# Head-output sums and values' low parts on GpSimd, and reordered steps beside the retention matmuls

## The chip, the cores and the metric

The kernel runs on one core of one Trainium2 chip. The time is the device time of one execution in microseconds (us); the kernel before takes 1518.18 us, the median of 3 runs (1517.76 to 1519.46). Engine names are those of the profile: PE (TensorE matmul, with PEld for its weight loads), DVE (VectorE), ACT (ScalarE), POOL (GpSimd) and SP (SyncE, which here only issues transfers).

## The reference

One layer of a hybrid model on a batch of 1: a feed-forward block, a mixer and a second feed-forward block, each behind an RMS norm and with a residual. The sequence has 512 tokens behind 16 meta tokens, the model width is 1024, everything is float32. The mixer adds two branches, each weighted with a sigmoid gate:

```
proj = u @ w_in          # split into rq, rk, rv, rg, aq, ak, av, iq, ik, iw, g_ret, g_att
rq = rope(rq); rk = rope(rk) * 256 ** -0.5            # 4 heads of 256, values of 512
yr = retention(rq, rk, rv)                            # decayed q k^T times v, RMS-normed per head
yr = (silu(rg) * yr) @ w_ret_out
qi, ki = rope(iq), rope(ik)                           # 8 index heads of 64, one key
score = sum_h wi[h] * relu(qi[h] @ ki)                # causal; the best 128 keys of each query
ya = dsa_attention(aq, ak, av, selected keys) @ w_att_out     # 8 heads of 128
merged = sigmoid(g_ret) * yr + sigmoid(g_att) * ya
return merged @ w_mix_out
```

The retention's recurrence over chunks equals one causal product with a matrix of decays, and the kernel computes it in that form.

## The kernel before

**Split matmuls.** Each float32 operand is split into a high part, rounded to the format that PE reads (`fp32r`), and a low part, the operand minus the high part. ACT writes the high part (`whi`, `vh`, `o`, `ikh`) and DVE the low one (`wlo`, `vl`, `ikl`). A product is three matmuls: high by high, high by low, low by high (`mm3`, L155).

**The order.** In the part that the change touches, the order on PE, DVE and ACT is the order in which the code is written. A list of steps (`more`) goes through a pipeline: each step is a weight tile, whose high part is made ahead of time and whose low part is made by `lower()`, and a function that emits the matmuls and then the work "beside" them. `between=((k, op), ...)` emits `op` before the k-th of the eight contraction steps of a projection; `behind` runs after it. An engine works through its own instructions in this order and stops at the first whose input is missing, so a late transfer or a long operation holds everything that is written behind it on that engine. SP and POOL issue transfers in their own written order. PSUM has two double banks and four single banks (`sm_tile`); a product waits when the banks have not been emptied.

**The retention stage** lies between 624 and 945 us of the span. Its steps are:

1. Gates 0 and 1 of the retention branch (`psgate`), with the loads of head 0 and of the index tables.
2. `decayed(0)`: query-key products of head 0 (`psst`), times the decay table (DVE, L1542), split into `ph` and `pl`. Its values are split by `values_in` (L1487 to L1493).
3. Projections of head 1's queries and keys (`psrq`, `psrk`). Beside the first lies `weigh_all(0)`: the products with the values (`pspv`, L1563, four blocks b of b + 1 key blocks), a sum of squares on ACT, and a product with the gate on DVE (`g<-pspv,g`, L1569). Each half of the result is normed and transposed in 32 x 32 blocks (`turn`), and goes through DRAM (`ots`) back into `land`.
4. Gates 2 and 3, with the index scores between them: one `pair` fills two banks with score products (`pssc`, L1315), followed by a relu on ACT into one of four `tmp` buffers (L1319) and a weighted sum on DVE (L1322). Their operands `iq`, `ikh` and `ikl` come from `index_queries` (four steps) and `index_keys` (three).
5. `arrived(0)` splits what landed into `o` (L322 and L323, one operation on each engine for each half).
6. Per head: `outputs(h)`, four steps of two products `psro` (one row block of `w_ret_out` each), added into eight accumulators `accr` in SBUF (L1694 to L1722; ACT copies for h = 0 at L1710, DVE adds otherwise at L1712). Inside the same steps lie `values_in(h+1)`, `decayed(h+1)` and `weigh_all(h+1)`. Then `queries_keys(h+2)` (L1663 to L1690) with the turned halves of head h+1, and so on. The last head has the projections of the attention's first key and query (`psak`, `psaq`) and gates 4 and 5 instead.
7. Between these, `pick(n)` emits n steps of the selection of the best keys, each a MAX (L1334) and a MATCH_REPLACE (L1335) on DVE over one score tile. There are 48 such steps in all.

The attention's heads come after it. For the last head the probabilities are transposed on PE (`psPT`, L1989 to L2002), split, and multiplied with the values (`weigh_v`, `psao`) inside the first column of the output projection (`psat`).

The lines that set the order of the retention stage:

```
more += queries_keys(1, (beside_q0, beside_q1, beside_k0, nothing), ((), (), (), ((7, pair),)))
five = tuple((i, pair) for i in (1, 2, 4, 5, 7))
more += steps_of(gr[2:4], [proj("psgate", REAL, five, after_2), proj("psgate", REAL, five, after_3)])
for h in range(1, RH - 1):
    more += outputs(h - 1, beside_outputs(h - 1))
    more += queries_keys(h + 1, (lambda h=h: (trip(h), pick(2)), lambda: pick(1), ...))
```

## Time and profile before

| | |
|---|---|
| median of 3 runs | 1518.18 us |
| the profiled execution's own time | 1518.44 us |
| its span | 1516.5 us |
| PE busy | 1483.9 us, 98% |
| DVE busy | 1143.6 us, 75% |
| ACT busy | 750.5 us, 49% |
| POOL busy | 192.7 us, 13% |
| mean granted clock of PE | 0.992 |
| retention, 600 to 950 us: PE, DVE, ACT, POOL busy | 330.4, 274.7, 169.9, 34.7 of 350 us |

A row of a timeline gives the start, the duration, the engine, the line and operation, what it writes and reads, its shape, a count where neighbours of one kind were joined, and in brackets the idle time before it with what ended it. A group row gives the same for all instructions of one kind: their number, then busy time and the mean of one in ns. Matmuls are pipelined: a duration of 0.39 us in a row stands beside starts that lie 0.23 us apart. A window row gives the busy times of the five engines, the mean granted clock of PE (1.00 is full), the busy share of the DMA engines and GB/s.

### The profile page before, as it was taken

The numbers are of one execution on the slowest core, as the hardware profiler recorded it, in microseconds if no ns is written. First come the engines' busy times: TensorE is split into PE (matmuls) and PEld (weight loads), VectorE is DVE, ScalarE is ACT, GpSimd is POOL, SyncE is SP. The second block draws the span as 40 slices with busy tenths as digits, with TensorE's granted clock in tenths as the row PEclk, the third lists the DMA queues.
The fourth block names the chain that finished last, engine by engine and source line by source line (L and its number), as shares of the span: only waits on it lengthen the run. The fifth ranks groups of instructions, "written<-read, shape, count | busy, mean of one in ns | idle before, by whom it ended". The sixth has DMA issues, their size and how long they took to land.

```text
span 1516.5 us, 22282 instructions
## 1 busy us (share of the span) xinstructions
PE 1483.9 (98%) x8704; PEld 1300.1 (86%) x8704; DVE 1143.6 (75%) x1715; ACT 750.5 (49%) x1054; POOL 192.7 (13%) x288
## 2 busy tenths in 40 slices
PE   9999999999999999989999999999999999999997
PEld 8999999999988778877878878989788888888886
DVE  5988586786887887477888878888557787777776
ACT  5555263455354444455543427677534644434343
POOL 1000000002100000210000002444202321111110
PEclk9999999999999999999999999999999999999999
DMA  5232323226654443544335344666657476466322
GB/s 169 69 123 85 116 90 106 97 89 214 220 169 142 157 166 120 197 149 150 114 136 171 114 149 121 172 178 178 208 164 261 150 228 205 127 206 198 123 84 110
DMA packets 185272, 228.41 MB, mean 151 GB/s; under 512 B 34768, under 2 KB 131560, under 8 KB 184912
## 3 DMA queue, kind: packets, MB, share of 16 engines
q1 hardware_dynamic: 164768, 173.97, 35.8%
q0 software_dynamic: 16288, 45.67, 10.3%
q10 hardware_dynamic: 4112, 7.36, 1.4%
q8 instruction: 68, 1.11, 0.3%
q14 instruction: 36, 0.29, 0.1%
HBM read 187.17 MB, written 39.60 MB: 150 GB/s over the span
## 4 chain that ended last, share of the span: by engine, by line
PE 86%; DVE 9%; ACT 3%; issue 2%; DMA 0%; POOL 0%; POOLq 0%; DVEq 0%; ACTq 0%
PE psd L155 8%; PE psd L2447 8%; PE psqX L2282 7%; PE psqX L155 7%; PE psvX L1196 7%; PE psvY L1196 4%; PE psqY L2282 4%; PE psqY L155 3%; PE psga L155 3%; PE psat L155 3%; PE psmo L155 3%; PE psak L155 3%; PE psaq L155 3%; PE psgate L155 2%; PE psrq L155 2%; PE psro L155 2%
## 5 line engine op out<-in xcount | busy, mean ns | idle before, releaser
L322 ACT ACTIVATE whi<-raw 128x1024 fp32r<-128x1024 f32 (+2 forms) x142 | 133.5, 941 | 125.0 <-PE psd L155 41.2
L323 DVE TENSOR_TENSOR wlo<-raw,whi 128x1024 fp32r<-128x1024 f32 (+2 forms) x142 | 155.8, 1100 | 34.0 <-ACT whi L322 34.0
L323 DVE TENSOR_TENSOR wlo<-w,whi 128x1024 fp32r<-128x1024 f32 x96 | 116.9, 1219 | 64.4 <-ACT whi L322 64.3
L322 ACT ACTIVATE whi<-w 128x1024 fp32r<-128x1024 f32 x96 | 101.5, 1058 | 110.1 <-PE psd L2447 39.3
L155 PE MATMUL psro<-o,whi 128*128 128x512 f32 x256 | 81.9, 400 | 6.5 <-DVE o L323 4.8
L155 PE MATMUL psd<-hl,whi 128*128 128x264 f32 x352 | 71.3, 284 | 0.0
L155 PE MATMUL psd<-hh,wlo 128*128 128x264 f32 x352 | 70.8, 283 | 0.0
L155 PE MATMUL psd<-hh,whi 128*128 128x264 f32 x352 | 70.7, 282 | 0.0
L155 PEld LDWEIGHTS psro<-o,whi 128*128 128x128 f32 x256 | 49.4, 193 | 18.6 <-DVE o L323 5.8
L115 ACT ACTIVATE whi<-raw 128x1024 fp32r<-128x1024 f32 (+1 forms) x42 | 43.5, 1036 | 42.4 <-PE psat L155 9.9
L155 PE MATMUL psqX<-tl,whi 128*128 128x264 f32 x216 | 61.1, 283 | 0.0
L155 PE MATMUL psqX<-th,whi 128*128 128x264 f32 x216 | 61.1, 283 | 0.0
L155 PE MATMUL psqX<-th,wlo 128*128 128x264 f32 x216 | 61.1, 283 | 0.0
L116 DVE TENSOR_TENSOR wlo<-raw,whi 128x1024 fp32r<-128x1024 f32 (+1 forms) x42 | 50.9, 1215 | 9.7 <-ACT whi L115 9.7
L2447 PE MATMUL psd<-whi,hl 128*128 128x512 f32 (+1 forms) x148 | 56.9, 384 | 0.0
L2447 PE MATMUL psd<-whi,hh 128*128 128x512 f32 (+1 forms) x148 | 56.8, 383 | 0.0
L2447 PE MATMUL psd<-wlo,hh 128*128 128x512 f32 (+1 forms) x148 | 56.7, 383 | 0.0
L155 PEld LDWEIGHTS psd<-hh,wlo 128*128 128x128 f32 x352 | 54.4, 188 | 0.0
L155 PEld LDWEIGHTS psd<-hh,whi 128*128 128x128 f32 x352 | 54.1, 188 | 0.0
L155 PEld LDWEIGHTS psd<-hl,whi 128*128 128x128 f32 x352 | 54.0, 188 | 0.0
L322 ACT ACTIVATE whi<-wsum 128x1024 fp32r<-128x1024 f32 x36 | 38.1, 1059 | 30.5 <-PE psd L155 15.0
L155 PE MATMUL psro<-o,wlo 128*128 128x512 f32 x128 | 50.9, 398 | 0.0
(566 smaller groups left out, 4701.5 us busy)
## 6 DMA issues: line engine op xcount, KB each, us to landing
w<-in_w_in_dram SPq DMA_DIRECT2D x40, 512.0 KB, 5.1
raw<-in_w_in_dram SPq DMA_DIRECT2D x27, 512.0 KB, 3.9
raw<-in_w_in_dram SPq DMA_DIRECT2D x13, 1024.0 KB, 6.0
raw<-in_ffn_w_down_dram SPq DMA_DIRECT2D x24, 512.0 KB, 4.0
raw<-in_ffn_w_up_dram SPq DMA_DIRECT2D x11, 1024.0 KB, 5.1
raw<-in_ffn_w_gate_dram SPq DMA_DIRECT2D x10, 1024.0 KB, 5.0
ws<-in_ffn_w_up_dram POOLq DMA_DIRECT2D x20, 512.0 KB, 6.4
w<-in_ffn_w_up_dram SPq DMA_DIRECT2D x20, 512.0 KB, 5.5
```

The costliest lines, as they stand in the source:

```text
L115: nc.scalar.activation(hi, src, AF.Copy)
L116: eng.tensor_tensor(lo, src, hi.bitcast(F32), ALU.subtract)
L155: nc.tensor.matmul(o, a[:, k, :], b[:, sl], start=first and k == 0 and i == 0, stop=last and k == nk - 1 and i == 2, skip_group_check=onto)
L322: nc.scalar.activation(hi, src, AF.Copy)
L323: return lambda: nc.vector.tensor_tensor(lo, src, hi.bitcast(F32), ALU.subtract)
L1196: nc.tensor.matmul(d[bank_][t], a, b[:, k, :], start=not onto and j + k + m == 0, stop=j + k == 3 and m == 2, skip_group_check=onto)
L2282: nc.tensor.matmul(ps[:, t], a, b[:, k, :], start=not onto and j + k + m == 0, stop=j + k == 3 and m == 2, skip_group_check=onto)
L2447: nc.tensor.matmul(ps, a, m[:, j, cs], start=first and i == 0, stop=last and i == 2)
```

## The change

1. **Index operands.** SP loads the index tables before the index queries' tile; the other four pieces of that tile are issued from POOL earlier. The multiplies and the addition of the index key, and its low part, go from DVE to POOL. The first two steps of `index_queries` are written right behind `decayed(0)`, the third beside head 1's second query projection, and the fourth ahead of the two rope steps beside the key projection.
2. **Values.** Head 0's values are split inside gate 1, before contraction step 4. For the other heads the low part is subtracted on POOL instead of DVE.
3. **Turns.** Two of the four transfers of each second half are issued from POOL.
4. **Accumulation.** Each `psro` bank is emptied by a copy on ACT, directly behind its matmuls and ahead of `lower()` and the steps beside. For h = 0 the copy goes into the accumulator; otherwise into one of two halves of `RR`, and POOL adds it to the accumulator.
5. **Scores and halves.** Score pairs begin inside the last key projection and lie at other contraction steps of gates 2 and 3. Both halves of head 0's `o` are split inside gate 2; both halves of heads 1 and 2 come beside the first key projection, with no selection step between; those of head 3 come inside gates 4 and 5.
6. **Selection.** The selection steps are distributed anew: before there were places for 54, so that the last places had none left; now there are places for 45, and the last three steps come at the end of the stage.
7. **Attention's end.** Three of the last head's four transposed blocks lie inside the projection before them, in free tiles, and the last weighing comes two contraction steps earlier in the first output column.

DVE around the weighing of head 0: before, from the last piece of the decays (`ptail`) on.

```order
L1379 TENSOR_TENSOR ptail<-tmp,ptail 16x512 [waits Activation_49]
L1493 TENSOR_TENSOR vl<-vl,vh 128x1024 [waits DMAHW1_49,Activation_49]
L1493 TENSOR_TENSOR vl<-vl,vh 128x1024 [waits DMAHW2_49,Activation_49]
L323 TENSOR_TENSOR wlo<-raw,whi 128x1024 [waits DMAHW7_49,Activation_49]
L1454 TENSOR_TENSOR tmp<-tmp,cos 64x512 [waits DMAHW6_49,DMASW5_49]
L1455 TENSOR_TENSOR tmp<-tmp,sin 64x512 [waits DMAHW7_49,DMASW7_49,DMASW6_49]
L1457 TENSOR_TENSOR tmp<-tmp 64x512 [waits DVE_49]
L1462 TENSOR_TENSOR ikl<-tmp,ikh 64x512 [waits Activation_49] x2
L1569 TENSOR_TENSOR g<-pspv,g 128x512 [waits Activation_49] x2
```

And in the changed kernel, from the same row:

```order
L1379 TENSOR_TENSOR ptail<-tmp,ptail 16x512 [waits Activation_49]
L1442 TENSOR_TENSOR ixs<-ixs,cos 128x4x384 [waits DMAHW7_49,DMAHW5_49]
L1442 TENSOR_TENSOR ixs<-ixs,sin 128x4x384 [waits DMASW4_49,DMASW3_49,DMAHW6_49,DMASW2_49,DMASW1_49]
L323 TENSOR_TENSOR wlo<-raw,whi 128x1024 [waits Activation_49]
L1570 TENSOR_TENSOR g<-pspv,g 128x512 [waits Activation_49] x2
L1574 TENSOR_SCALAR osum<-osum 128x2
```

`vl` now stands ahead of the decays, the index key is gone from DVE, and the two multiplies of the index queries (`ixs`), which wait for transfers, stand ahead of the weights' low part and of the gate products that empty the `pspv` banks.

ACT in the outputs of head 1, with the last rope pieces of head 2's keys and head 2's values and decays: before, no copy of a `psro` bank is on ACT here.

```order
L322 ACTIVATE rqk<-tmp 128x528
L322 ACTIVATE whi<-raw 128x1024
L322 ACTIVATE rqk<-tmp 128x528
L1491 ACTIVATE vh<-vraw 128x1024 x2
L322 ACTIVATE whi<-raw 128x1024
L1498 ACTIVATE g<-g 128x1024 x2
L322 ACTIVATE ph<-tmp 128x512
```

In the changed kernel:

```order
L1712 ACTIVATE RR<-psro 128x512
L322 ACTIVATE rqk<-tmp 128x528
L1712 ACTIVATE RR<-psro 128x512
L322 ACTIVATE whi<-raw 128x1024
L1712 ACTIVATE RR<-psro 128x512
L322 ACTIVATE rqk<-tmp 128x528
L1712 ACTIVATE RR<-psro 128x512
L1491 ACTIVATE vh<-vraw 128x1024 x2
L322 ACTIVATE whi<-raw 128x1024
L1712 ACTIVATE RR<-psro 128x512
L1499 ACTIVATE g<-g 128x1024 x2
L1712 ACTIVATE RR<-psro 128x512
```

A copy now stands ahead of a high part of the weights each time, and one copy stands behind the two Silu passes (`g<-g`). POOL's additions follow these copies one for one, with the two low parts of the values after the fourth.

DVE beside the first key projection of head 2, with head 1's landed halves: before, from the second rope piece on.

```order
L323 TENSOR_TENSOR rqk<-tmp,rqk 128x512 [waits Activation_49]
L323 TENSOR_TENSOR o<-land,o 128x4x256 [waits DMAHW0_49,Activation_49]
L1334 MAX top<-score_6588 128x8
L1335 MATCH_REPLACE score_6588<-top,score_6588 128x512 [waits DVE_49]
L1334 MAX top<-score_6588 128x8 [waits DVE_49]
L1335 MATCH_REPLACE score_6588<-top,score_6588 128x512 [waits DVE_49]
L323 TENSOR_TENSOR wlo<-raw,whi 128x1024 [waits PE_49,Activation_49]
L323 TENSOR_TENSOR o<-land,o 128x4x256 [waits DMAHW1_49,Activation_49]
```

In the changed kernel:

```order
L323 TENSOR_TENSOR wlo<-raw,whi 128x1024 [waits DMAHW1_49,Activation_49]
L323 TENSOR_TENSOR o<-land,o 128x4x256 [waits DMAHW4_49,Activation_49]
L323 TENSOR_TENSOR o<-land,o 128x4x256 [waits DMAHW5_49,Activation_49]
L323 TENSOR_TENSOR rqk<-tmp,rqk 128x512 [waits DVE_49]
L1519 TENSOR_TENSOR tmp<-tmp 128x512 [waits DVE_49]
L323 TENSOR_TENSOR rqk<-tmp,rqk 128x512 [waits Activation_49]
L323 TENSOR_TENSOR wlo<-raw,whi 128x1024 [waits PE_49,Activation_49]
```

Both halves now stand next to each other, ahead of the last rope pieces and of the selection steps.

The diff, cut to its core:

```diff
         def bring_index():
-            nc.sync.dma_start(ia[:, :, :NL], fq[:, :, :NL])
-            for r in range(4):
-                o = r ^ 1
-                nc.gpsimd.dma_start(ib[32 * r : 32 * r + 32, :, :NL], fq[32 * o : 32 * o + 32, :, :NL])
             for i, t in enumerate((cosi, sini)):
                 nc.sync.dma_start(t, rope[0, i, :, REAL])
+            nc.sync.dma_start(ia[:, :, :NL], fq[:, :, :NL])
...
+            PT = nc.gpsimd.tensor_tensor
             if i == 0:
-                TT(a, a, cosi[:64], ALU.mult)
-                TT(b, b, sini[:64], ALU.mult)
-            elif i == 1:
-                TT(a, a, b, ALU.add)
+                PT(a, a, cosi[:64], ALU.mult)
+                PT(b, b, sini[:64], ALU.mult)
+                PT(a, a, b, ALU.add)
...
+            low = nc.gpsimd.tensor_tensor if h else TT
             for i in range(2):
-                TT(lo[i].bitcast(F32R), lo[i], hi[:, 2 * i : 2 * i + 2].bitcast(F32), ALU.subtract)
+                low(lo[i].bitcast(F32R), lo[i], hi[:, 2 * i : 2 * i + 2].bitcast(F32), ALU.subtract)
...
-                nc.sync.dma_start(d.rearrange("(b i) a e -> a i b e", i=32)[a],
+                eng = nc.gpsimd if half and a > 1 else nc.sync
+                eng.dma_start(d.rearrange("(b i) a e -> a i b e", i=32)[a],
...
             def k0(ps):
                 pss["ka"] = ps
+                asides[2]()
                 some(ropes["q"], 2)
-                asides[2]()
...
-                        if j == 0:
-                            lower()
-                            beside(i)
                         a = acc_r[2 * i + j]
                         if h == 0:
                             nc.scalar.activation(a, ps, AF.Copy)
                         else:
-                            TT(a, ps, a, ALU.add)
+                            t = RR[:, j * S : (j + 1) * S]
+                            nc.scalar.activation(t, ps, AF.Copy)
+                            nc.gpsimd.tensor_tensor(a, a, t, ALU.add)
+                        if j == 0:
+                            lower()
+                            beside(i)
...
-                pick((1, h == 0, 1 + (h == 0), 2 + (h == 0))[i])
+                pick((1, 1, 0, 1)[i])
...
-            values_in(0)
+            index_queries(0)
+            index_queries(1)
+            index_keys(0)
...
-            proj("psgate", REAL, (), after_1)(w, lower)
+            proj("psgate", REAL, ((4, lambda: values_in(0)),), after_1)(w, lower)
...
-        more += queries_keys(1, (beside_q0, beside_q1, beside_k0, nothing), ((), (), (), ((7, pair),)))
-        five = tuple((i, pair) for i in (1, 2, 4, 5, 7))
-        more += steps_of(gr[2:4], [proj("psgate", REAL, five, after_2), proj("psgate", REAL, five, after_3)])
+        more += queries_keys(1, (beside_q0, beside_q1, beside_k0, nothing), ((), (), (), ((3, pair), (7, pair))))
+        come = [(i, lambda half=half: arrived(0, (half,))) for half, i in enumerate((2, 6))]
+        more += steps_of(gr[2:4], [proj("psgate", REAL, (*come, *((i, pair) for i in (1, 3, 5, 7))), later_gate(2)),
+                                   proj("psgate", REAL, tuple((i, pair) for i in (0, 2, 4, 6, 7)), after_3)])
...
-            more += queries_keys(h + 1, (lambda h=h: (trip(h), pick(2)), lambda: pick(1), lambda h=h: (arrived(h, (0,)), pick(2)),
-                                           lambda h=h: (arrived(h, (1,)), pick(2))))
+            more += queries_keys(h + 1, (lambda h=h: (trip(h), pick(3)), lambda: pick(1), lambda h=h: arrived(h), lambda: pick(2)))
...
-        more += steps_of(gr[4:6], [proj("psgate", REAL, (), lambda ps: (later_gate(4)(ps), arrived(p, (0,)), pick(4))),
-                                   proj("psgate", REAL, (), lambda ps: (later_gate(5)(ps), arrived(p, (1,)), pick(4)))])
+        more += steps_of(gr[4:6], [proj("psgate", REAL, ((6, lambda: arrived(p, (0,))),), lambda ps: (later_gate(4)(ps), pick(2))),
+                                   proj("psgate", REAL, ((2, lambda: arrived(p, (1,))),), lambda ps: (later_gate(5)(ps), pick(3)))])
...
-                    wide_gate()
+                    ends = last_tiles()
+                    wide_gate(between=[(3 + i, lambda kb=kb: transpose_block(kb, ends[kb])) for i, kb in enumerate((0, 1, 3))])
...
-                between=((KD - 1, lambda: weigh_v(AH - 1, pend, vs[AH - 1])),))
+                between=((KD - 3, lambda: weigh_v(AH - 1, pend, vs[AH - 1])),))
```

More of the change, by code (lines that the diff above doesn't have):

```diff
@@ L1862, with gate_a @@
     ga = Cols(w_in, OFF_GA, KD, step=1)
-    def gate_a(ps):
-        mm3([(ps, REAL)], ga.next(), xs, KD)
+    def gate_a(ps, between=()):
+        mm3([(ps, REAL)], ga.next(), xs, KD, between=between)
         t = tp["pool"].tile([P, S], F32, tag="gate", name="gate", bufs=2)
@@ L1987, in weigh_turned, with transpose_block, transpose_tail @@
                 split(*(t.rearrange(f"p ({o}) -> p a j c", a=4, j=4) for o, t in zip(("a j c", "j a c", "j a c"), (ps, *ao_parts[h]))))
[L1989 to L1997 removed]
+            def transpose_block(kb, parts):
+                ps = sm_tile("psPT")
+                for j in range(kb, 4):
+                    nc.tensor.transpose(ps[:, j * P : (j + 1) * P], prob[j][:, NM + kb * P : NM + (kb + 1) * P], ident)
+                split(ps[:, kb * P :], *parts)
+            def transpose_tail():
                 ps = sm_tile("psPT")
@@ L2001, in transpose_p, with last_tiles @@
                 split_rows(ps[:NM], tp["p"], "hlh")
-                return parts
+            def transpose_p():
+                parts = [part_tiles(kb, S - kb * P) for kb in range(4)]
+                for kb in range(4):
+                    transpose_block(kb, parts[kb])
+                transpose_tail()
+                return parts
+            def last_tiles():
+                a, b = ([at.tile([P, n], F32R, tag=f"a{t}{i}", name="ptx") for i in range(2)] for t, n in (("q", S), ("k", TX)))
+                return [a, [t[:, : S - P] for t in b], part_tiles(2, 2 * P), [t[:, S - P : S] for t in b]]
             def weigh_v(h, parts, v):
@@ L2012, in weigh_v, with wide_gate @@
                 split(ps, *ao_parts[h])
-            def wide_gate(tile=None):
+            def wide_gate(tile=None, between=()):
                 if gr.at < gr.n:
@@ L2017, in wide_gate @@
                 else:
-                    t = gate_a(tile or mm_tile("psga")[:, :S])
+                    t = gate_a(tile or mm_tile("psga")[:, :S], between)
                     nc.sync.dma_start(gd[KD + ga.at - 1], t)
```

39 lines of the change are left out of this document (15 added, 24 removed).

## The prediction

> **What bounds the kernel now.** I read four views in this order: the totals and the chain of waits, to see which engine sets the end; what TensorE (PE) waited for in the stage that the change rewrites; the granted clock there; and single rows on DVE, ACT and POOL for prices. First the totals and the chain:
>
> ```profile
> PE 1483.9 (98%) x8704; PEld 1300.1 (86%) x8704; DVE 1143.6 (75%) x1715; ACT 750.5 (49%) x1054; POOL 192.7 (13%) x288
> ...
> PE 86%; DVE 9%; ACT 3%; issue 2%; DMA 0%; POOL 0%; POOLq 0%; DVEq 0%; ACTq 0%
> ```
>
> PE is the bound, and no matmul is added or dropped. So the change can gain only PE's idle time and matmuls that ran at a reduced clock. The whole span has 1516.5 - 1483.9 = 32.6 us idle. The next view lists the waits of PE from 600 to 950 us, where the retention stage lies (columns: engine, tile and line of the waiting matmul, what released it, sum of us, count, longest):
>
> ```profile
> PE psro L155 <- DVE o L323: 4.8, 3, 2.0
> PE pssc L1315 <- DVE iq L1449: 3.2, 2, 2.1
> PE pssc L1315 <- ACT tmp L1319: 2.8, 1, 2.8
> PE psst L1538 <- DVE accr L1712: 1.7, 2, 1.4
> PE psro L155 <- ACT o L322: 1.7, 1, 1.7
> PE psst L1538 <- ACT accr L1710: 1.4, 1, 1.4
> PE pspv L1563 <- ACT vh L1491: 1.2, 1, 1.2
> PE pspv L1563 <- DVE vl L1493: 0.8, 1, 0.8
> PE pspv L1563 <- DVE accr L1712: 0.7, 2, 0.5
> PE pspv L1563 <- DVE g L1569: 0.6, 1, 0.6
> ```
>
> These sum to 18.9 us, and every one has an edit aimed at it. Now the stretches around the long waits (columns: busy of PE, weight load, DVE, ACT, POOL, then PE's granted clock, DMA share, GB/s):
>
> ```profile
> 644.00:656.00 12.00, 9.39 (x33) 6.68 (x31) 7.93 (x10) 8.20 (x13) 0.83 (x1) 0.86 0.65 210
> ...
> 676.00:684.00 8.00, 4.82 (x16) 3.33 (x15) 6.15 (x5) 6.01 (x7) 0.00 (x0) 0.79 0.06 9
> ...
> 884.00:896.00 12.00, 8.90 (x27) 6.55 (x26) 11.45 (x32) 2.56 (x3) 0.55 (x1) 0.72 0.42 153
> ...
> 692.00:704.00 12.00, 9.18 (x41) 7.73 (x40) 8.34 (x12) 7.83 (x13) 0.58 (x1) 0.86 0.06 22
> ...
> 700.00:950.00 250.00, 238.98 (x1211) 200.77 (x1211) 208.47 (x387) 117.94 (x178) 19.83 (x32) 0.98 0.45 141
> ```
>
> The clock is below full in the first four. Length times (1 - clock) is what was lost: 12 x 0.14 = 1.7, 8 x 0.21 = 1.7, 12 x 0.28 = 3.4 and 12 x 0.14 = 1.7, together 8.5 us. Single rows show what such a loss looks like, and where it doesn't come:
>
> ```profile
> 679.20 0.50 PE L1315 MATMUL pssc<-ikh,iq 128*128 128x512 f32 x1 [2.12 <-DVE iq L1449]
> ...
> 680.99 0.80 PE L1315 MATMUL pssc<-ikh,iq 128*128 128x512 f32 x1 [1.06 <-DVE iq L1449]
> ...
> 682.01 0.63 PE L155 MATMUL psgate<-xh,whi 128*128 128x512 f32 x1
> ...
> 766.71 0.50 PE L155 MATMUL psro<-o,whi 128*128 128x512 f32 x1 [1.96 <-DVE o L323]
> 767.05 0.40 PE L155 MATMUL psro<-o,wlo 128*128 128x512 f32 x1
> ```
>
> After 3.2 us of idle close together a matmul of 512 columns took 0.63 us; after one idle of 1.96 us it still took 0.40. The four stretches hold 2.0 to 3.2 us of idle close together (the waits of the list, added by place). So a removed wait is worth more than its length where idle time is dense. The Trainium skill (TensorE: Matmul & The Clock Gate, the part on the clock gate) says that an idle window of about 3.4 us, free-running, halves the clock; by it alone a stage with idle below that keeps its clock, and the clock losses here could also fall elsewhere in a run. The rows agree in that one idle of 1.96 us cost nothing; they differ in that losses came below 3.4 us of idle. I count the clock as recoverable, and keep the other case as a rival.
>
> **The change, place by place.** DVE, ACT and POOL prices first, from groups and single rows (start, duration, engine, line, operation):
>
> ```profile
> L1712 DVE TENSOR_TENSOR accr<-psro,accr 128x512 f32<-128x512 f32 x16 | 10.2, 681 | 0.0
> L1493 DVE TENSOR_TENSOR vraw<-vraw,vh 128x1024 fp32r<-128x1024 f32 x6 | 7.1, 1217 | 0.0
> L1710 ACT ACTIVATE accr<-psro 128x512 f32<-128x512 f32 x8 | 4.4, 586 | 0.9 <-PE psro L155 0.9
> L1396 POOL TENSOR_TENSOR accr<-accr,gate 128x512 f32<-128x512 f32 x8 | 11.2, 1394 | 37.3 <-DMA gate<-gd 20.8 <-ACT gate L2026 9.0 <-ACT gate L1392 7.5
> ...
> 648.96 0.83 POOL L1330 COPY bias<-caus 128x128 f32<-128x128 f32 x1 [7.95 <-DMA caus<-in_causal_dram]
> ...
> 647.28 2.36 DVE L1493 TENSOR_TENSOR vl<-vl,vh 128x1024 fp32r<-128x1024 f32 x2 [4.24 <-ACT vh L1491]
> ...
> 663.39 1.72 DVE L1442 TENSOR_TENSOR ixs<-ixs,cos 128x1536 f32<-128x1536 f32 x1
> 665.03 1.75 DVE L1442 TENSOR_TENSOR ixs<-ixs,sin 128x1536 f32<-128x1536 f32 x1
> ...
> 645.47 0.39 PE L155 MATMUL psrq<-xl,whi 128*128 128x512 f32 x1
> 645.70 0.39 PE L155 MATMUL psrq<-xh,wlo 128*128 128x512 f32 x1
> ...
> 658.75 0.40 PE L155 MATMUL psrq<-xh,whi 128*128 128x512 f32 x1
> ```
>
> Work moved: DVE loses 24 accumulations (24 x 0.68 = 16.3 us) and six low parts (6 x 1.22 = 7.3). ACT gains 24 copies (24 x 0.59 = 14.2), hidden while ACT is busy 117.9 of 250 us. POOL gains 24 x 1.39 = 33.4 and six low parts; the trace has no 128x1024 on POOL, so I take twice 1.39, 2.8 each, 16.7 together (bounds 1.39, and 3.0 by the slowest 128x512 shown below). That is 50 us on an engine busy 19.8 of those 250. It is hidden unless a copy has to wait for its half of RR. Five index-key operations of 64x512 go to POOL too; I cost them at nothing, since POOL is busy 0.83 of 12 us in the first stretch and the first score comes 20 us later; without that cover the scores would wait for them.
>
> A, head 0's weighing (644 to 660). Splitting the values inside gate 1 removes the waits on vh and vl (1.2 + 0.8) and, with them, the 1.7 of clock. But DVE's queue now holds the two index multiplies (1.72 + 1.75) and the weights' low part (1.22, row in D) ahead of the first g, and they wait for index loads. The table issued just behind those loads landed at 648.96, the latest row for them; the queries' own tile now comes third, and I take 647 for it (an estimate, two us ahead of that row since its bytes stand ahead of the table's). Then the first g is done at 647 + 3.5 + 1.2 + 0.7 = 652.4. PE would reach block 3 of the weighing at 650.8: the waits end, four matmuls of block 0, seven and ten more, at the 0.23 us by which the two psrq rows follow each other, from 645.9. It waits 1.6, finishes block 3 (13 x 0.23 = 3.0) at 655.4 and starts the next projection 3.3 us sooner than at 658.75. Bounds: 4.9 with no wait; 1.3 if the load comes at 648.96. I take 3.3.
>
> B, first index scores (676 to 684). The queries' multiplies are done about 12 us sooner, and their low parts stand ahead of the rope steps. Both waits (3.2) and the 1.7 of clock go; the moved steps may hold the rope pieces by up to 1.7 on DVE, in front of matmuls of a later head: I take 4.7, bounds 1.5 (the clock stays) and 4.9.
>
> C, gates 2 and 3 (692 to 704). The 2.8-us wait sat behind DVE's two halves of `o`, 2.36 us in one piece, so ACT could not refill its four temporaries. Now the halves go in one at a time between score pairs. DVE still has 4 x 1.22 of weights, 2.4 of halves and 24 weighted sums in about 19 us of PE work, so I expect 1.0 left: 2.8 + 1.7 - 1.0 = 3.5, bounds 1.0 and 4.5.
>
> D, the gaps of 0.3 to 2.0 us between outputs and heads. What is left of the list of waits is psro <- DVE o without its last (4.8 - 1.4 = 3.4), psst and pspv <- accr (1.7 + 1.4 + 0.7 = 3.8): 7.2 us. The rows behind the largest of them:
>
> ```profile
> 764.30 1.22 DVE L323 TENSOR_TENSOR wlo<-raw,whi 128x1024 fp32r<-128x1024 f32 x1
> 765.43 1.22 DVE L323 TENSOR_TENSOR o<-land,o 128x1024 fp32r<-128x1024 f32 x1
> ```
>
> The second half was queued behind three selection steps; both halves now stand ahead of them. ACT's copies free a bank without DVE's selection in front of it, but one bank still waits behind two Silu passes. I take 6.0 of 7.2, bounds 3 and 7.2.
>
> E, the last head (884 to 896): two waits of 1.7 and 1.4 and 3.4 of clock, 6.5. The halves move into gates 4 and 5, several us ahead of their use, and two of the second turn's four transfers leave SP's queue for POOL's, where at most one addition of 1.39 stands ahead of them. I take 6.0, bounds 3.1 and 6.5.
>
> F, the attention tail, from these PE rows:
>
> ```profile
> 1084.17 0.60 PE L2000 MATMUL psPT<-ident,pj 128*16 128x128 f32 x4 [0.92 <-DVE ptl L116]
> ...
> 1092.53 0.50 PE L155 MATMUL psat<-vo,whi 128*128 128x512 f32 x1 [0.69 <-ACT vo L115]
> 1093.26 0.50 PE L155 MATMUL psat<-vo,whi 128*128 128x512 f32 x1 [0.22 <-DVE vo L116]
> ```
>
> Three of the transposes now lie inside a projection, and the last weighing is two steps earlier: 1.4 of 1.8, bounds 0 and 1.8.
>
> The sum is 3.3 + 4.7 + 3.5 + 6.0 + 6.0 + 1.4 = 24.9. Against it stands what POOL does to DVE, from rows of DVE and then POOL:
>
> ```profile
> 951.74 2.19 DVE L116 TENSOR_TENSOR wlo<-raw,whi 128x1024 fp32r<-128x1024 f32 x1
> ...
> 951.35 1.50 POOL L1294 TENSOR_TENSOR tmp<-tmp,sin 128x512 f32<-128x512 f32 x1 [1.80 <-DVE cross L1953]
> ```
>
> The split that elsewhere takes 1.22 took 2.19 beside 1.1 us of POOL's multiply: almost the whole overlap is lost. POOL's new 50 us over PE's 250 would meet DVE operations that read two SBUF tiles for about 40% of the time (weights, halves, rqk and low parts), and cost 50 x 0.4 x 0.9 = 18 us of DVE. DVE is relieved of 23.6, so it stays below its 208 of 250; but single late splits will come. I charge one new idle of the present mean, 18.9 / 15 counted waits = 1.3, and one clock loss of 1.7, together 3. The Trainium skill (GPSIMD Engine Reference, specifications and key points) speaks against this change: the two engines share their SBUF interfaces when DVE has two SBUF inputs, and it puts elementwise work on POOL at about half DVE's rate. The trace agrees on both (2.19 for 1.22, 1.39 against 0.68), and by that page alone the move would gain nothing on DVE; the gains above come mostly from order, not from DVE's total.
>
> So 24.9 - 3 = 22 us. Against the profiled execution's own 1518.44 (span 1516.5 and 1.9 around it), within 0.3 of the median shown, that gives 1496.5; I round to **1497**.
>
> **Rivals.** First, the idle moves instead of going: A's load comes at 648.96 or later and the wait before g keeps its clock loss, C stays bound by DVE, D gives half. With the lower bounds of A to F, 1.3 + 1.5 + 1.0 + 3.0 + 3.1 + 0 = 9.9, the time is about 1508. DVE's 83% of 700 to 950 us speaks for it; against it, the waits sit behind named operations that leave.
>
> Second, the clock windows stay though the waits are shorter: 24.9 - 8.5 - 3 = 13.4, about 1505. A new idle of 1.6 us in A after the present dense stretch would be where it starts; the 1.96 us without loss speaks against it.
>
> Third, no net change. POOL's 18 us of stretch all land before PE (bank-emptying copies, RR halves and splits), and eat the 22: 1514 to 1520. That needs DVE to be the bound nearly throughout; it has more than 20 us of reserve per 250.
>
> Fourth, **slower**: the copy of output pair i waits on ACT until POOL's addition has read RR's half. Each copy now stands ahead of the weight splits in ACT's queue, so a POOL queue that is late by x makes ACT, the weights and PE late by x. It decides once POOL needs more than PE's time for an output: 12 matmuls of 0.23 = 2.7 us against 1.39, or 2.8 after a low part. Two low parts (5.6) sit in POOL's queue between the fourth and fifth addition of each of two heads, and the copy after next would wait 5.6 + 1.39 - 2 x 2.7 = 1.6 there. If each of the 24 copies waited that much, 24 x 1.6 = 38 against 24.9 of gain: 1518.4 + 13 = 1531. Only three such places have low parts, so it needs POOL twice as slow as in its rows.
>
> **How the numbers follow.** Forecast 0.58; idle moved 0.18; clock stays 0.10; no net change 0.07; slower 0.07. The first three are faster by over 0.2% (3 us, about what a measurement of this kernel can tell from no change), and so lies their sum, 0.86; the rest is shared as 0.07 and 0.07. The forecast's upper gain is the sum of the upper bounds, 4.9 + 4.9 + 4.5 + 7.2 + 6.5 + 1.8 = 29.8, which gives 1488.6. For the low end I take 1489, for the high end 1509, which takes in the first two rivals.
>
> **What would show it.** Right: PE's idle between 600 and 950 below 4 us, the clock 1.00 in 676 to 704 and 884 to 896, no psro wait on `o`, no psst wait on an accumulation. For A: a wait of pspv on g of 1 to 2 us before block 3. Wrong: a clock below 0.9 in any of the four stretches, ACT waiting on POOL's accr rows, DVE's splits above 1.6 us in the outputs, or pspv waiting on the index multiplies for over 2.5 us. A PE busy sum above 1484 would mean slower matmuls, which nothing here counts on.

## The result and the profile after

The changed kernel takes 1495.57 us (median of 4 runs, 1494.3 to 1496.16) against 1518.82 us before (4 runs, 1517.76 to 1519.65): a ratio of 0.9846, 95% interval 0.9829 to 0.9863. The forecast was 1497 in a range of 1489 to 1509. The profiled execution took 1496.16 us, its span is 1494.4.

First its totals and its chain of waits (shares of the span by engine):

```profile
PE 1476.2 (99%) x8704; PEld 1296.7 (87%) x8704; DVE 1130.1 (76%) x1680; ACT 761.6 (51%) x1078; POOL 261.9 (18%) x331
...
PE 92%; DVE 3%; DMA 2%; ACT 2%; issue 1%; POOL 0%; POOLq 0%; ACTq 0%; SPq 0%; DVEq 0%
```

PE's idle time fell from 32.6 to 18.2 us, and its busy time by 7.7 us with the same 8704 matmuls. Most of the latter is clock: 8.5 us were lost in the retention stage before, 1.8 now. DVE's busy time fell by only 13.5 us, though work of 27 us left it (16.3 of accumulations, 7.3 of low parts, 3.4 of the index key). The waits of PE between 600 and 950 us:

```profile
PE pspv L1564 <- DVE g L1570: 2.9, 1, 2.9
PE psst L1539 <- DVE tmp L1543: 1.0, 1, 1.0
PE pssc L1315 <- ACT wt L1302: 0.9, 1, 0.9
PE pssc L1315 <- ACT tmp L1319: 0.7, 1, 0.7
```

Every wait on `o`, on an accumulation, and on `vh` and `vl` is gone, and those on `iq` are down from 3.2 to 0.2 us. One new wait stands out: 2.9 us on `g`. The window view shows where the time went (PE, weight load, DVE, ACT, POOL, granted clock, DMA share, GB/s):

```profile
644.00:656.00 12.00, 9.22 (x41) 7.29 (x39) 9.40 (x9) 7.76 (x13) 6.99 (x8) 1.00 0.77 258
656.00:676.00 20.00, 19.84 (x118) 17.80 (x119) 13.63 (x19) 10.14 (x13) 6.91 (x9) 0.91 0.57 153
...
700.00:950.00 250.00, 249.27 (x1305) 212.96 (x1304) 211.04 (x398) 141.07 (x221) 86.97 (x78) 1.00 0.50 156
```

From 700 to 950 us PE stops for 0.7 us in all; before it stopped for 11. The weighing of head 0 still has its stop, and the 656 to 676 window lost 20 x 0.09 = 1.8 us of clock behind it. Its rows on PE and DVE (start, duration, and in brackets the idle time before with its releaser):

```profile
656.16 0.80 PE L1564 MATMUL pspv<-vh,ph 128*128 128x512 f32 x1 [2.94 <-DVE g L1570]
656.75 0.63 PE L1564 MATMUL pspv<-vl,ph 128*128 128x512 f32 x1
...
649.78 1.76 DVE L1442 TENSOR_TENSOR ixs<-ixs,cos 128x1536 f32<-128x1536 f32 x1 [1.93 <-DMA ixs<-fq]
651.46 1.85 DVE L1442 TENSOR_TENSOR ixs<-ixs,sin 128x1536 f32<-128x1536 f32 x1
653.23 2.28 DVE L323 TENSOR_TENSOR wlo<-raw,whi 128x1024 fp32r<-128x1024 f32 x1
655.43 1.27 DVE L1570 TENSOR_TENSOR g<-pspv,g 128x512 f32<-128x512 f32 x2
...
651.66 2.76 POOL L1457 TENSOR_TENSOR tmp<-tmp 64x512 f32<-64x512 f32 x1
```

DVE stood 1.93 us for the index load, and the weights' split then took 2.28 us beside POOL's 2.76-us addition of the index key, where it takes 1.22 alone.

The table gives the time by place: how much later (+) or sooner (-) a kernel passes each stretch than the kernel before, from the start times of the same matmuls in both traces. A runs from the first gate to head 1's second query projection, B and C from there to the first output, D to gate 4, E to gate 6, F to the end of the span. The runs below are in it.

| kernel | A | B, C | D | E | F |
|---|---|---|---|---|---|
| predicted | -3.3 | -8.2 | -6.0 | -6.0 | -1.4 |
| changed | +0.9 | -7.2 | -8.9 | -6.5 | -1.4 |
| changed, again | -0.9 | -7.2 | -8.9 | -6.5 | -0.9 |
| index_behind | -3.2 | -3.0 | -8.9 | -6.5 | -2.2 |
| index_between | -2.8 | -3.0 | -8.9 | -6.5 | -2.4 |
| between_psw | -3.8 | -2.0 | -8.9 | -6.5 | -2.0 |
| iq_early | -3.8 | -5.0 | -8.9 | -6.5 | -1.8 |
| accr_dve | -0.6 | -7.2 | -8.9 | -6.5 | +3.9 |
| accr_late | -0.8 | -7.2 | -0.4 | -6.5 | -1.4 |
| halves_old | -0.7 | -4.2 | -3.7 | -0.2 | -2.4 |
| vl_dve | -0.9 | -7.3 | -7.5 | -6.5 | -2.3 |
| attn_old | +0.8 | -7.2 | -8.9 | -6.5 | +0.5 |
| relief_alone | +1.6 | -0.6 | 0.0 | -2.7 | +0.2 |
| halves_alone | 0.0 | +1.3 | -5.5 | -6.5 | +7.3 |

B to E repeat within 0.1 us wherever their code is the same. A and F do not. Seven of the traces have the changed kernel's code in A (both of the changed kernel, `accr_dve`, `accr_late`, `halves_old`, `vl_dve`, `attn_old`), and in all seven the load of the index queries lets DVE start 23.9 to 24.3 us behind the first gate. Five of them have an A of -0.6 to -0.9. The other two, at +0.8 and +0.9, lost clock behind the wait on `g`. F varies from -0.9 to -2.4 us with the same code, and why is open. The spans start up to 1.5 us apart ahead of A, in code that no run touches.

### The profile page after: what moved, and what is told of

Read it like the earlier page. It is cut to its first block, busy times and chain, and to the rows that moved or that the text cites. A ratio compares the mean times of both kernels' runs of the same rounds, so it can differ in the third digit from the quotient of the medians.

```text
span 1494.4 us, 22333 instructions
## 1 busy us (share of the span) xinstructions
PE 1476.2 (99%) x8704; PEld 1296.7 (87%) x8704; DVE 1130.1 (76%) x1680; ACT 761.6 (51%) x1078; POOL 261.9 (18%) x331
## 4 chain that ended last, share of the span: by engine, by line
PE 92%; DVE 3%; DMA 2%; ACT 2%; issue 1%; POOL 0%; POOLq 0%; ACTq 0%; SPq 0%; DVEq 0%
PE psd L155 8%; PE psqX L2293 7%; PE psd L2458 7%; PE psqX L155 7%; PE psvX L1196 7%; PE psro L155 6%; PE psvY L1196 4%; PE psqY L2293 4%; PE psqY L155 3%; PE psat L155 3%; PE psmo L155 3%; PE psak L155 3%; PE psaq L155 3%; PE psrk L155 2%; PE psgate L155 2%; PE psrq L155 2%
## 5 line engine op out<-in xcount | busy, mean ns | idle before, releaser
L323 DVE TENSOR_TENSOR wlo<-raw,whi 128x1024 fp32r<-128x1024 f32 (+2 forms) x142 | 160.2, 1131 | 36.3 <-ACT whi L322 36.0
L155 PE MATMUL psro<-o,whi 128*128 128x512 f32 x256 | 78.9, 389 | 0.0
L287 POOL TENSOR_TENSOR RR<-RR,sq 128x528 f32<-128x528 f32 x7 | 9.4, 1336 | 324.0 <-ACT sq L286 324.0
L2256 POOL DMA_DIRECT2D hts<-cross x40 | 26.0, 658 | 166.5 <-DVE cross L2253 166.4
```

Source lines behind the costliest of these rows:

```text
L155: nc.tensor.matmul(o, a[:, k, :], b[:, sl], start=first and k == 0 and i == 0, stop=last and k == nk - 1 and i == 2, skip_group_check=onto)
L287: eng.tensor_tensor(ssum[:, :n], ssum[:, :n], sq[:, :n], ALU.add)
L323: return lambda: nc.vector.tensor_tensor(lo, src, hi.bitcast(F32), ALU.subtract)
L2256: nc.gpsimd.dma_start(d.rearrange("(b i) a e -> a i b e", i=32)[a], cross[32 * a : 32 * a + 32].rearrange("p b c t -> p b (c t)"))
```

## The experiments

Two theories stood against each other. By the first, **order**, the gain comes from which operation stands first in DVE's and ACT's queues. By the second, **load**, it comes from the work taken off DVE. Each run changes the changed kernel, or, where said, the kernel before. Each ratio is to the kernel before on the same chip.

**The accumulations back on DVE.**

```diff
-                            t = RR[:, j * S : (j + 1) * S]
-                            nc.scalar.activation(t, ps, AF.Copy)
-                            nc.gpsimd.tensor_tensor(a, a, t, ALU.add)
+                            TT(a, ps, a, ALU.add)
```

> The changed kernel with the 24 accumulations back on DVE, each one DVE addition out of the bank, but still written directly behind the matmuls, ahead of the weights' split and the side work. Theory (order: what counts is that the bank is emptied first): DVE takes 16.3 us more of additions and is spared the stretch by POOL, and the time rises by 0 to 3 us, to 1495.6 to 1498.6. Rival (load: the gain between the heads comes from relieving DVE): the waits of PE on DVE between 700 and 870 us come back, 7 to 9 us, and the time is 1502 to 1505.

1499.81 us, ratio 0.9890 (0.9871 to 0.9910). The time lies between the two theories; by the ratios it is 6.7 us more than the changed kernel's, which is in the rival's range. But the rival's mechanism is not what happened. By the table, through the heads (D, E) nothing is lost, and PE does not stop between 700 and 880 us. Everything is lost in F, at the first attention head. Windows and PE's rows:

```profile
700.00:880.00 180.00, 180.00 (x927) 153.15 (x926) 152.51 (x266) 81.93 (x119) 30.50 (x27) 1.00 0.50 161
...
903.51 0.63 PE L1924 MATMUL psS<-ak,aq 128*128 128x400 f32 x2 [1.49 <-ACT aq L115]
904.86 1.92 PE L1924 MATMUL psS<-ak,aq 128*128 128x400 f32 x13 [0.71 <-DVE aq L116]
916.54 0.96 PE L1995 MATMUL psPT<-ident,pj 128*16 128x128 f32 x4 [2.89 <-DVE ptl L116]
...
890.00:902.00 12.00, 12.00 (x54) 9.61 (x52) 11.79 (x29) 5.29 (x8) 2.69 (x8) 1.00 0.56 158
```

The selection steps that the heads had no room for have piled up to here: DVE is busy for 11.79 of 12 us, and the last of the 48 steps begins 6.7 us after gate 6, in the changed kernel 1.9 us after it. The first attention query is late behind them. So the relief of DVE is worth nothing where it is given, and some 5 us at the end of the queue.

**The first copy of a pair late again.**

```diff
+                        if j == 0:
+                            lower()
+                            beside(i)
                         a = acc_r[2 * i + j]
...
-                        if j == 0:
-                            lower()
-                            beside(i)
```

> The changed kernel with copies on ACT and additions on POOL as in it, but the first copy of each pair again behind the weights' split and the side work, as before the change. Theory (order): three waits of psst on a late bank come back, 1.4 us each and 0.25 us for each restart, and the time rises by 3 to 5 us, to 1498.5 to 1500.6. Rival (load): DVE is relieved as much as in the changed kernel, and the time stays within 1 us of 1495.6.

1502.54 us, ratio 0.9904 (0.9886 to 0.9922), by the ratios 8.8 us more. Order is right in kind, and twice too small: of D's 8.9 us only 0.4 is left. The three stops of PE in D came to 4.6 us (0.49, 2.12 and 1.97). The rest is mostly clock, 6 x 0.28 + 8 x 0.21 = 3.4 us, which the expectation had left out:

```profile
778.00:784.00 6.00, 5.99 (x25) 4.28 (x26) 5.69 (x8) 2.00 (x5) 4.84 (x3) 0.72 0.00 0
840.00:848.00 8.00, 8.00 (x33) 5.69 (x32) 6.44 (x9) 3.66 (x7) 4.16 (x4) 0.79 0.38 126
```

The rows around head 2's products:

```profile
778.01 4.55 PE L1539 MATMUL psst<-rqk 128*128 128x256 f32 x18 [2.12 <-DVE tmp L1543]
...
774.57 2.78 DVE L323 TENSOR_TENSOR wlo<-raw,whi 128x1024 fp32r<-128x1024 f32 x1 [1.71 <-ACT whi L322]
777.27 1.14 DVE L1543 TENSOR_TENSOR tmp<-psst,u 128x512 f32<-128x512 f32 x2
...
774.43 2.00 ACT L1499 ACTIVATE g<-g 128x1024 f32<-128x1024 f32 x2
776.32 1.08 ACT L1715 ACTIVATE RR<-psro 128x512 f32<-128x512 f32 x2
...
773.83 5.77 POOL L1494 TENSOR_TENSOR vraw<-vraw,vh 128x1024 fp32r<-128x1024 f32 x2
```

Both copies now stand behind the Silu passes, so two banks instead of one are held until 776.9 and 777.4 us, and the split that DVE does meanwhile takes 2.78 us beside POOL. The wait is named after DVE, since that came last. How the 2.12 us divide between the late copies and the late split is not shown; the edit moves nothing but the copies and the additions that follow them.

**The halves and the selection steps where they were.**

```diff
-... lambda: pick(1), lambda h=h: arrived(h), lambda: pick(2)))
+... lambda: pick(1), lambda h=h: (arrived(h, (0,)), pick(2)), lambda h=h: (arrived(h, (1,)), pick(2))))
...
-... proj("psgate", REAL, ((6, lambda: arrived(p, (0,))),), lambda ps: (later_gate(4)(ps), pick(2))),
+... proj("psgate", REAL, (), lambda ps: (later_gate(4)(ps), arrived(p, (0,)), pick(4))),
...
                 pss["ka"] = ps
-                asides[2]()
                 some(ropes["q"], 2)
+                asides[2]()
```

> The changed kernel with the turned halves of heads 1 to 3 and the selection steps where they were before the change (halves in two places with selection steps between, those of head 3 behind gates 4 and 5; the side work of the first key projection again behind the two rope steps). Theory (order): the psro waits on o return, 1.96, 1.43, 1.70 and 1.39 us with 0.25 us for each restart and 3.4 us of clock, and the time rises by 9 to 11 us, to 1504.5 to 1506.5. Rival (load): with DVE relieved of the accumulations the halves are split early enough wherever they stand, at most the last head's 3.1 us come back without the clock loss, and the time is 1496 to 1499.

1505.98 us, ratio 0.9924 (0.9904 to 0.9944), as order has it; by the ratios it is 11.8 us more than the changed kernel, a little over the 9 to 11 expected. Its psro waits are those of the kernel before to the tenth, although DVE is relieved:

```profile
PE psro L155 <- DVE o L323: 4.8, 3, 2.0
PE pssc L1315 <- DVE iq L1449: 2.5, 2, 1.5
PE psst L1539 <- DVE tmp L1543: 1.8, 1, 1.8
PE psro L155 <- ACT o L322: 1.7, 1, 1.7
```

The wait on `iq` shows that the swap of the side work and the two rope steps, small as it is, carries 3.0 us of B and C here, in part clock (0.94 from 676 to 706 us).

**Each theory alone, on the kernel before.** First the load alone: ACT's copies and POOL's additions where DVE's additions stood, and the low parts on POOL. Then the order of the halves, the side work and the selection alone (the reverse of the diff of the run before, on the kernel before). The first one's edit:

```diff
-                            TT(a, ps, a, ALU.add)
+                            t = RR[:, j * S : (j + 1) * S]
+                            nc.scalar.activation(t, ps, AF.Copy)
+                            nc.gpsimd.tensor_tensor(a, a, t, ALU.add)
...
+            low = nc.gpsimd.tensor_tensor if h else TT
             for i in range(2):
-                TT(lo[i].bitcast(F32R), lo[i], hi[:, 2 * i : 2 * i + 2].bitcast(F32), ALU.subtract)
+                low(lo[i].bitcast(F32R), lo[i], hi[:, 2 * i : 2 * i + 2].bitcast(F32), ALU.subtract)
```

> The kernel before with one part of the change: accumulations as copies on ACT and additions on POOL, at the place where DVE's additions stood, and the low parts of the values of heads 1 to 3 on POOL; all else as before. Theory (order): what waits on o, iq, vh and the relu buffers is untouched; at most the waits on accr go (1.7 and 0.7 us, with 0.25 us of restart each), so the time falls by 0 to 4 us. Rival (load): DVE sheds 16.3 and 7.3 us in the heads, so the waits on o shrink too, and the time falls by 8 to 12 us.

> The kernel before with one part of the change: the turned halves of heads 1 to 3 in one place, those of head 3 inside gates 4 and 5, the side work of the key projection ahead of the two rope steps, and the selection steps as in the changed kernel. Theory (order): the waits on o go (1.96, 1.43, 1.70, 1.39 us), with 0.25 us of restart each and 3.4 us of clock; the time falls by 9 to 12 us. Rival (load): with the accumulations still on DVE the halves are late wherever they stand, and the time falls by 0 to 5 us.

The load alone gives 1519.25 us, ratio 1.0008 (0.9999 to 1.0017): no change. The halves alone give 1514.12 us, ratio 0.9973 (0.9963 to 0.9983): less than order expected. The table again splits it: from the first output to gate 6 they gain 12.0 us, as forecast, 1.3 are given back in B and C, where the swap alone does not help, and 7.3 in F. The waits in F are the same three as with the accumulations on DVE, and the clock fell around them in two places (0.72 from 916 to 922 and from 930 to 936 us, 3.4 us together). The profiled execution took 1515.92 us, 1.8 above the median, so 7.3 is more than the usual loss:

```profile
PE pssc L1315 <- ACT tmp L1319: 3.0, 2, 2.8
PE psPT L1999 <- DVE ptl L116: 2.9, 1, 2.9
...
PE psS L1926 <- ACT aq L115: 1.5, 1, 1.5
...
PE psS L1926 <- DVE aq L116: 0.7, 1, 0.7
```

Both theories are needed then. In the heads (D, E) order makes the gain, and the accumulations' move off DVE keeps it from being lost once the selection steps no longer fill the waits. For A to C the experiments settle less: no run takes back the index key's move to POOL, or the halves inside gate 2.

**The low parts of the values back on DVE.**

```diff
-            low = nc.gpsimd.tensor_tensor if h else TT
+            low = TT
```

> The changed kernel with the six low parts of the values of heads 1 to 3 back on DVE. Theory (order): DVE had room there, since even with the accumulations on DVE PE did not stop once between 700 and 880 us; the time is unchanged, 1495 to 1497. Rival (load): decays of the next head are late by up to 2.4 us for each of three heads, and the time rises by 3 to 7 us.

1495.79 us, ratio 0.9859 (0.9840 to 0.9878): not to be told from the changed kernel. D loses 1.5 us, where D otherwise repeats within 0.1. That part of the change is worth about that much in D.

**The last attention head as before.**

```diff
-                    ends = last_tiles()
-                    wide_gate(between=[(3 + i, lambda kb=kb: transpose_block(kb, ends[kb])) for i, kb in enumerate((0, 1, 3))])
+                    wide_gate()
...
-                    pend = ends
-                    transpose_block(2, ends[2])
-                    transpose_tail()
+                    pend = transpose_p()
...
-                between=((KD - 3, lambda: weigh_v(AH - 1, pend, vs[AH - 1])),))
+                between=((KD - 1, lambda: weigh_v(AH - 1, pend, vs[AH - 1])),))
```

> The changed kernel with the last attention head as before the change: all transposes behind the second gate, the last weighing one contraction step before the end. Theory: the waits of PE on the last transposes and on vo return, 1.4 to 1.8 us, with 0.25 us of restart for each of three: 1496.8 to 1498.2. Rival (these waits are hidden by what the retention stage gave up): unchanged, within 0.5 us of 1495.6 in the profile's span.

1496.72 us, ratio 0.9863 (0.9846 to 0.9879), an interval that overlaps the changed kernel's. The trace shows the expected waits:

```profile
1062.58 0.60 PE L1997 MATMUL psPT<-ident,pj 128*16 128x128 f32 x4 [0.93 <-DVE ptl L116]
1070.92 0.49 PE L155 MATMUL psat<-vo,whi 128*128 128x512 f32 x1 [0.69 <-ACT vo L115]
1071.64 0.50 PE L155 MATMUL psat<-vo,whi 128*128 128x512 f32 x1 [0.23 <-DVE vo L116]
```

These are 1.85 us; in the changed kernel one wait of 0.46 stands in their place, 0.79 in its second profile, so 1.1 to 1.4 is gained.

**The new wait on `g`: four tries.** First the two multiplies go behind the weighing.

```diff
             open_gates(0)
-            index_queries(0)
-            index_queries(1)
...
         def beside_q0():
             weigh_all(0)
+            index_queries(0)
+            index_queries(1)
```

> The changed kernel with one edit: the two multiplies of the index queries are written behind the weighing of head 0, not ahead of it. Theory (order on DVE: the multiplies wait for their transfer and hold the products that empty the pspv banks): the 2.9 us wait of PE on g falls to 0 to 1.6 us and the clock loss behind it goes, so the time falls by 2 to 4.6 us from 1495.6, to 1491 to 1493.6. Rival (the index chain is needed early, and whatever is late moves on): the first scores wait 2 to 4 us more for iq instead, and the time stays within 1 us of 1495.6.

1495.61 us, ratio 0.9858 (0.9842 to 0.9874): the rival. A is 2.3 to 4.1 us better than in the two profiles of the changed kernel, and B and C lose 4.2 of theirs: the scores wait 2.6 us for `iq`, and the clock falls behind it (0.89 from 676 to 706 us, 3.3 us lost). In the second try the first two `g` stand ahead of the weights' split, and the multiplies behind the third `g`; the third try adds the earlier transposes of the index weights.

```diff
-                lower()
+                if picks.pop("hold", None):
+                    picks["lower"] = lower
+                else:
+                    lower()
                 behind(ps)
...
                 weigh(h, b)
+                if h == 0 and b == 1:
+                    picks.pop("lower")()
+                if h == 0 and b == 2:
+                    index_queries(0)
+                    index_queries(1)
...
             open_gates(0)
-            index_queries(0)
-            index_queries(1)
             index_keys(0)
+            picks["hold"] = True
...
             index_keys(1)
+            picks["pairs"] = index_steps()
...
             index_queries(3)
-            picks["pairs"] = index_steps()
...
-queries_keys(1, (beside_q0, beside_q1, beside_k0, nothing), ((), (), (), ((3, pair), (7, pair))))
+queries_keys(1, (beside_q0, beside_q1, beside_k0, nothing), ((), (), ((6, pair),), ((7, pair),)))
```

The moved line with `index_steps` and the last pair of lines are the third try alone.

> The changed kernel with the first two products of head 0's weighing with its gate, g, ahead of the next weights' split on DVE, and the two multiplies of the index queries behind the third g and ahead of the transposes. Theory (order on DVE): the 2.9 us wait of PE on g goes with its clock loss, and since the multiplies run while DVE would wait for the normed half, iq is not late either: the next projection starts 3 to 4.7 us sooner and the first output starts as much sooner, so the time is 1491 to 1492.6. Rival (the index chain has no slack): the scores wait for iq as with the multiplies behind the whole weighing, 2.6 us, and the time stays within 1 us of 1495.6.

> As the run before, and in addition the three small transposes of the index weights inside the first key projection, so that ACT's copy wt stands ahead of the second rope piece. Theory: the 0.85 us wait of the scores on wt goes with 0.25 us of restart: 1 us less than the run before. Rival: the scores then wait for iq or for a relu buffer in its place, and the two runs are equal within 0.5 us.

1496.88 us (0.9863, 0.9849 to 0.9878) and 1494.64 us (0.9848, 0.9833 to 0.9862): neither is to be told from the changed kernel. In both traces the scores wait 3.6 us for `iq`, and the clock falls behind that wait (0.94 and 0.89 from 676 to 706 us). The wait on `wt` is in neither, hidden behind the longer one; so what the earlier transposes are worth stays open. The fourth try puts `iq` ahead of the weights' split:

```diff
-queries_keys(1, (beside_q0, beside_q1, beside_k0, nothing), ((), (), ((6, pair),), ((7, pair),)))
+queries_keys(1, (beside_q0, beside_q1, beside_k0, nothing), ((), (), ((0, lambda: index_queries(3)), (6, pair)), ((7, pair),)))
```

> The kernel with the products g ahead, the index multiplies between and the weights' transposes earlier (the two runs before), and with the low parts of the index queries, iq, ahead of the next weights' split on DVE, where DVE waited 2.8 us for ACT. Theory (order on DVE): iq is done 3 us sooner, so the 3.6 us wait of the scores and its clock loss (about 1.8) go, and the span is 4 to 5.5 us shorter than the 1494.3 of the run before: 1489 to 1490.5, with times of 1491 to 1492.5. Rival (ACT or POOL is next): the low part of the key on POOL or the high parts on ACT hold the first score by as much, and the span is 1493 or more.

> The changed kernel, unedited, beside the others on one chip: 1493 to 1497, with a wait of PE on g between 1.3 and 2.9 us, depending on when the index transfers land.

1492.91 us, ratio 0.9836 (0.9822 to 0.9849), beside 1493.96 us, ratio 0.9842 (0.9828 to 0.9855), for the unedited changed kernel on the same chip. The span is 1491.0 against 1492.9: between the two expectations, and the times can't be told apart. The rival names what came next:

```profile
674.35 0.50 PE L1315 MATMUL pssc<-ikl,iq 128*128 128x512 f32 x1 [1.73 <-POOL ikl L1462]
...
668.65 4.53 DVE L1449 TENSOR_TENSOR iq<-ixs,iq 64x1536 fp32r<-64x1536 f32 x2
673.21 2.17 DVE L323 TENSOR_TENSOR wlo<-raw,whi 128x1024 fp32r<-128x1024 f32 x1
...
669.33 4.97 POOL L1462 TENSOR_TENSOR ikl<-tmp,ikh 64x512 fp32r<-64x512 f32 x2 [3.84 <-ACT ikh L1460]
```

`iq` on DVE and the key's low part on POOL now run at the same time; in the changed kernel they took 3.54 and 2.64 us, here 4.53 and 4.97. The key, not the query, is what the scores wait for. Whether its low part would do better back on DVE was not tried.

## Why the prediction was right, and where not

**The sum.** 22 us were forecast; the profiled execution is 22.3 us shorter, the medians 23.3. The sum holds better than its terms, and that is luck in part: in this profile A, B and C fell short by 5.2 us, D and E exceeded their terms by 3.4, and the 3 us charged against POOL covered the rest. The signs that were named ahead say the same. No `psro` wait on `o` and no `psst` wait on an accumulation is left, and the clock is 1.00 in 676 to 704 and 884 to 896. But PE's idle time from 600 to 950 us is 6.4 us and not below 4, PE waited 2.9 us on `g` where over 2.5 was a sign of being wrong, and three splits in the outputs took more than 1.6 us (1.70, 2.01, 2.00), though PE was not held by them.

**A failed**, and with it the weighing's bound of 1.3 from below: +0.9 and -0.9 us in the two profiles of the changed kernel, not -3.3. The step is "I take 647 for it". The load of the index queries, issued third, was put at two us ahead of the table behind it; it released DVE at 649.78, and the table's row came at 650.38, 0.6 us later. The stage begins 1.1 us later in this span, so the load was 1.6 us later than assumed. A second term was not in the sum, the split beside POOL (2.28 for 1.22). The two make the first `g` 2.5 us late against the forecast, so -3.3 becomes -0.8, and the five traces that kept their clock show -0.6 to -0.9. A third term was missing and is not in that difference: the low parts of the values now stand ahead of the decays on DVE, and PE waits 1.0 us at `psst`. That only brings PE later to the same late `g`: in `accr_late` PE waits 1.8 us at `psst` and 1.3 on `g`, and its A is -0.8. The rest, 1.7 us, is clock, and whether it is lost does not follow from the length of the wait. `accr_dve` waited exactly as long as the changed kernel and kept its clock:

```profile
655.11 0.50 PE L1564 MATMUL pspv<-vh,ph 128*128 128x512 f32 x1 [2.94 <-DVE g L1570]
655.44 0.40 PE L1564 MATMUL pspv<-vl,ph 128*128 128x512 f32 x1
```

The waits on `vh` and `vl` did go. The form of the failure was named ahead: "the load comes at 648.96 or later and the wait before g keeps its clock loss". One number behind B is off by its own rows: the multiplies were to end at 650.5 instead of 666.8, which is 16 us sooner and not 12. Nothing in the sum hangs on it.

**B and C** came out at 7.2 of 8.2 us: the scores kept waits of 0.9 on `wt`, which nobody had foreseen, 0.7 on a relu buffer and 0.2 on `iq`, with the clock at 1.00.

**D was too small**: 8.9 us, more than the 7.2 of its idle time, of which 6.0 were forecast. The mechanism was right, the term mis-sized: all the waits went, and a stop costs more than its idle time. D held seven waits, and (8.9 - 7.2) / 7 is 0.25 us for each. The bound "3 and 7.2" left that out. The halves carry 5.3 of it by `halves_old`, and 5.5 by `halves_alone`. `accr_late` loses 8.5, but that is not the share of the banks: its copies wait behind the Silu passes on ACT, where the kernel before had additions on DVE, and 3.4 of it is clock.

**E and F** were right: 6.5 for 6.0, with the clock at 1.00, and 1.0 to 1.4 in F by the waits (the span's end gives 0.9 and 1.4).

**POOL's charge** of 3 us was right in kind and wrong in place. DVE is stretched, by about half of the 18 us: groups of DVE rows over the four heads, before (700 to 880 us) and after (695 to 866), show it. First before:

```profile
L323 DVE TENSOR_TENSOR pl<-tmp,ph 128x512 fp32r<-128x512 f32 x3 | 2.1, 693 | 0.7 <-ACT ph L322 0.7
...
L323 DVE TENSOR_TENSOR wlo<-raw,whi 128x1024 fp32r<-128x1024 f32 x24 | 29.2, 1221 | 6.0 <-ACT whi L322 6.0
```

and after, with POOL's own groups of the stage:

```profile
L323 DVE TENSOR_TENSOR wlo<-raw,whi 128x1024 fp32r<-128x1024 f32 x24 | 31.9, 1332 | 9.8 <-ACT whi L322 9.5
...
L323 DVE TENSOR_TENSOR pl<-tmp,ph 128x512 fp32r<-128x512 f32 x3 | 3.6, 1201 | 1.8 <-ACT ph L322 1.7
L323 DVE TENSOR_TENSOR pl<-tmp,ph 128x384 fp32r<-128x384 f32 x3 | 3.2, 1060 | 0.0
...
L1713 POOL TENSOR_TENSOR accr<-accr,RR 128x512 f32<-128x512 f32 x24 | 38.0, 1588 | 65.2 <-ACT RR L1712 65.0
L1494 POOL TENSOR_TENSOR vraw<-vraw,vh 128x1024 fp32r<-128x1024 f32 x6 | 17.4, 2920 | 12.6 <-ACT vh L1491 12.6
```

POOL's operations took 1.59 and 2.92 us for the 1.39 and 2.8 assumed. In the heads this cost PE nothing; it cost where DVE's next result was awaited, at `g`. The slower rival's sign, ACT held by POOL's additions, is in none of ACT's waits between 640 and 905 us. The only wait of a copy on its half of RR is on a gate's transfer out of the same tile, and PE was not held by it:

```profile
ACT RR L1712 <- DMA gd<-RR: 3.4, 1, 3.4
```

**What the forecast did not see** is what the relief of DVE does. It was counted as a reserve against POOL's stretch. Alone it is worth nothing (1.0008), and without it some 5 to 7 us of the order's gain are lost at the first attention head, far behind most of the places where they were made. By the table the accumulations are the part that counts there; the low parts of the values back on DVE cost nothing in F.

## What to carry to other kernels

Where an engine runs in written order, look first at what stands ahead of the operation that PE waits for; here a relief of the engine changed nothing until the order did. Then look at where the work displaced by the new order piles up. An operation that waits for a transfer holds what stands behind it, but moving it back pays only if its own result has slack: here the wait went from `g` to `iq`. A load's landing needs a row of its own: the guess from the row of its neighbour was 1.6 us off. Compare profiles by stretches between the same matmuls: a gain of 12 us and a loss of 7 us show there, where the total shows 4.

## What the runs showed of the hardware

- POOL's two-input operations and DVE's two-input operations from SBUF stretch each other: 0.69 to 1.20 us (`pl`, 128x512), 1.22 to 2.28 and 2.78 (`wlo`), and POOL's own 2.64 to 4.97 (`ikl`). The Trainium skill (GPSIMD Engine Reference, specifications) names this case, with no size for it. In the rows around `g` the one that began first was hardly stretched, and the others ended in turn: DVE's multiply, begun 0.2 us ahead of POOL's addition, took 1.85 us (1.75 before) and ended at 653.31, the addition at 654.42, DVE's split at 655.51. DVE rows that read a bank beside SBUF do not stretch: in the rows of `accr_late` two `tmp<-psst,u` took 1.14 us, and all of it lay beside POOL's low parts; before the change two took 1.15 (787.38 us).
- A stop of PE costs about 0.25 us more than its idle time, from D above. The rows around one of them agree. Running, these matmuls start 0.23 us apart; here 2.36 and 0.34 us lie between the starts, which is 2.24 more than two such steps, with 1.96 idle:

```profile
764.35 0.40 PE L155 MATMUL psro<-o,whi 128*128 128x512 f32 x1
766.71 0.50 PE L155 MATMUL psro<-o,whi 128*128 128x512 f32 x1 [1.96 <-DVE o L323]
767.05 0.40 PE L155 MATMUL psro<-o,wlo 128*128 128x512 f32 x1
```

- The length of one idle time does not say whether PE's clock falls. Behind the wait on `g` it fell after 2.94 us in the changed kernel (0.63 us for a matmul of 0.39) and after 2.65 in `attn_old`; it held after 2.94 in `accr_dve`, 2.57 in the changed kernel's second profile, and, before the change, after 1.96 at a `psro` wait. The Trainium skill (TensorE: Matmul & The Clock Gate, the part on the clock gate) puts the window at about 3.4 us, free-running; the losses here came below that length, and that the same idle time had both outcomes agrees with a window that does not start with the idle time.
